# Staged weight loads, earlier LayerNorm statistics and a finer end in a two-layer encoder trunk

## The chip, the cores and the metric

The kernel runs on one core of a Trainium2 chip. The metric is the device time of one execution in microseconds (us). The kernel before took 2858.91 us in the median of three runs (2856.44 to 2863.42).

The core has a matrix engine (TensorE, PE), three engines for elementwise work (VectorE or DVE, ScalarE or ACT, GpSimd or POOL), and SyncE (SP), on whose queue this kernel issues its transfers. Each engine takes its instructions strictly in its own order, and waits on semaphores for the others.

## The reference

Two groups of rows, a prompt of 1024 tokens and a sample of 512, go through the same two layers of width 1024, and a last RMSNorm.

- Layer 0: RMSNorm, one input projection (`w_in_mix`), bidirectional retention with 4 heads beside differential attention with 8 heads, both gated, joined to 2048 columns, an output projection (`w_out_mix`, 2048 x 1024), and a residual.
- Layer 1: RMSNorm, a projection to three parts of 2048 (`w_in_conv`), then

```python
glu = a * jax.nn.sigmoid(b)
y = conv(glu, conv_w, width 31, depthwise) + conv_b
y = jax.nn.silu(layer_norm(y, cn_g, cn_b)) * jax.nn.silu(gate)
return x + y @ w_out          # w_out_conv, 2048 x 1024
```

The LayerNorm runs over the 2048 channels, so its statistics are known only when the last channel has been convolved.

## The kernel before, in words

All 1536 rows stay on one core. Matrix products keep the accuracy of float32 by splitting both factors into a high part, rounded to the matrix engine's format, and a low part, the rest: three matmuls (high by high, high by low, low by high) add into one PSUM tile of 128 x 512. ACT makes a high part by a cast, DVE or POOL the low part by a subtraction. That is true of weights and of activations.

The program is recorded by a layer that puts each instruction behind the ones it depends on and sorts by priority; `weave(spread(M), steps)` mixes a list of matrix work M with steps placed at fractions of its length (0 to 1). What the recording gives is a fixed order for each engine. A buffer of a pool is reused when all that reads it has run, so a load into one may stand in SP's queue and hold up all loads behind it.

The stages that the change touches, in order of time:

- **Attention output** (`oproj_steps`, L769 to L771). Each of twelve row tiles has a "slab" of 1 MB, the attention results, which SP loads. For four row tiles the first eight k (WA) are multiplied while the last head's job still runs, for the others (itemsB) behind it; the second eight k (WB) follow. `load_wout` loads the weights in pieces of 128 x 512 through three "wr" buffers, and splits each (L741 cast, L743 subtraction: DVE for WA, POOL for WB). "T1", "T2" and the like are big buffers of the head that serve as slabs.
- **Retention head** just before: vst are the rotated queries and keys (L384 to L386 on DVE), which free the PSUM tile "pp" for the next projection (L191 to L193). dmt are decay tables on DVE.
- **Convolution.** Sixteen channel tiles of 128 channels. `conv_setup` (L1209) loads the 31 weights of each channel through three "sg" buffers and transposes them on PE. The taps run on DVE (L1138). s1 and s2 hold the sums over channels of y and its square, added tile by tile on POOL (L1159, L1163).
- **LayerNorm.** `ln_cols` (L1264 to L1273) turns s1 and s2 by PE transposes, reduces them on DVE, and makes mu and vr, the reciprocal deviation (POOL's pow). `ln_rows` (L1281, L1282) spreads them back over the partitions, by four transposes each and ACT copies. Meanwhile PE runs the last gate projections, whose results ACT passes on with Silu (L1095, sg).
- **Output phase.** Three groups g of four row tiles t. Operand k of a group, z, is made by `z_make`: three DVE operations, Silu and cast on ACT, zl on POOL (L1315 to L1322). Five operands are kept (NZ). The products (L1364 to L1366, oc) run k by k over the four row tiles for the first KT of sixteen k, so that all eight PSUM banks fill at once, and then tile by tile for the rest, with the last RMSNorm behind each (`finish`, `finish_last`). The weights of `w_out_conv` (W1, W2) are loaded and split on POOL during group 0.

## Time and profile before

| what | us |
|---|---|
| median of three runs | 2858.91 (2856.44 to 2863.42) |
| profiled execution | 2858.97 |
| its span | 2857.0 |
| PE busy | 2801.6 (98%) |
| DVE, ACT, POOL busy | 1766.5, 1137.4, 1218.3 |

The span runs from the first to the last recorded instruction; 1.97 us lie around it. Start times count from the span's start. In a row of the timeline stand start, duration, engine, line, operation, output and input tiles, and in brackets the idle time ahead of it and what ended that. A row of waits tells who waited, for whom, how long in total, how often, and the longest.

### The profile page before, as it was taken

The numbers are of one execution on the slowest core, as the hardware profiler recorded it, in microseconds if no ns is written. First come the engines' busy times: TensorE is split into PE (matmuls) and PEld (weight loads), VectorE is DVE, ScalarE is ACT, GpSimd is POOL, SyncE is SP. The second block draws the span as 40 slices with busy tenths as digits, with TensorE's granted clock in tenths as the row PEclk, the third lists the DMA queues.
The fourth block names the chain that finished last, engine by engine and source line by source line (L and its number), as shares of the span: only waits on it lengthen the run. The fifth ranks groups of instructions, "written<-read, shape, count | busy, mean of one in ns | idle before, by whom it ended". The sixth has DMA issues, their size and how long they took to land.

```text
span 2857.0 us, 36862 instructions
## 1 busy us (share of the span) xinstructions
PE 2801.6 (98%) x13342; PEld 2314.7 (81%) x13342; DVE 1766.5 (62%) x3112; ACT 1137.4 (40%) x2124; POOL 1218.3 (43%) x1198
## 2 busy tenths in 40 slices
PE   7999999999999999999999999999999999999998
PEld 6788888888888778888878788788888888887787
DVE  4222336777777786665241143699899999965653
ACT  4233245555555665654332033333232323334321
POOL 4244343333333435555634000466565655556331
PEclk9999999999999999999999999999999999999999
DMA  4121222111111213333366653011221121255442
GB/s 132 46 64 51 59 67 76 55 52 55 55 55 51 81 51 95 98 102 98 98 209 208 209 177 113 25 56 58 65 72 59 51 81 63 74 173 178 161 144 81
DMA packets 283574, 264.32 MB, mean 93 GB/s; under 512 B 14636, under 2 KB 231908, under 8 KB 283264
## 3 DMA queue, kind: packets, MB, share of 16 engines
q1 hardware_dynamic: 283392, 261.96, 29.3%
q8 instruction: 105, 1.72, 0.2%
q14 instruction: 77, 0.63, 0.1%
HBM read 192.64 MB, written 69.27 MB: 92 GB/s over the span
## 4 chain that ended last, share of the span: by engine, by line
PE 89%; DMA 4%; DVE 2%; issue 2%; POOL 1%; ACT 1%; SPq 0%; DVEq 0%; POOLq 0%; ACTq 0%
PE pp L193 19%; PE pp L191 19%; PE pp L192 19%; PE pp L769 2%; PE pp L771 2%; PE pp L770 2%; PE sc L616 2%; PE sc L618 2%; PE tr L656 2%; PE oc L1366 2%; PE oc L1364 2%; PE oc L1365 2%; DMA wr<-in_w_out_mix 1%; PE o L673 1%; PE o L674 1%
## 5 line engine op out<-in xcount | busy, mean ns | idle before, releaser
L191 PE MATMUL pp<-hw,wh 128*128 128x512 f32 x2112 | 866.6, 410 | 1.3 <-DVE vst L386 0.9
L193 PE MATMUL pp<-hw,wl 128*128 128x512 f32 x2112 | 829.2, 393 | 0.0
L192 PE MATMUL pp<-hw,wh 128*128 128x512 f32 x2112 | 827.5, 392 | 0.0
L169 POOL TENSOR_TENSOR wl<-wr,wh 128x512 fp32r<-128x512 f32 x320 | 460.1, 1439 | 688.3 <-ACT wh L168 666.2
L193 PEld LDWEIGHTS pp<-hw,wl 128*128 128x128 f32 x2112 | 397.0, 188 | 88.1 <-issue 0.9
L191 PEld LDWEIGHTS pp<-hw,wh 128*128 128x128 f32 x2112 | 397.8, 188 | 77.8 <-issue 1.7
L192 PEld LDWEIGHTS pp<-hw,wh 128*128 128x128 f32 x2112 | 398.4, 189 | 73.1 <-issue 0.9
L168 ACT CAST wh<-wr 128x512 fp32r<-128x512 f32 x320 | 197.2, 616 | 552.2 <-PE pp L192 433.3
L620 DVE CUSTOM_DVE_ANT_0 st<-sc,W 128x512 f32<-128x512 f32 x320 | 208.9, 686 | 64.0 <-PE sc L618 54.4
L1138 DVE SCALAR_TENSOR_TENSOR acc<-xs,wS,acc 128x777 f32<-128x777 f32 x240 | 246.1, 1025 | 1.4
L1138 DVE SCALAR_TENSOR_TENSOR acc<-X,wE,acc 128x777 f32<-128x777 f32 x240 | 246.1, 1025 | 0.6
L631 ACT ACTIVATE st<-st,nm 128x1024 f32<-128x1024 f32 (+1 forms) x192 | 192.3, 1003 | 40.9 <-DVE nm L620 20.8
L1117 POOL TENSOR_TENSOR pa<-pa,ct 128x777 f32<-128x777 f32 x96 | 179.9, 1874 | 5.9
L659 ACT CAST ah<-tr 128x512 fp32r<-128x512 f32 x160 | 93.3, 584 | 171.8 <-PE tr L656 170.5
L193 PE MATMUL pp<-h2b,wl 128*128 128x512 f32 x384 | 152.4, 397 | 0.0
L191 PE MATMUL pp<-h2b,wh 128*128 128x512 f32 x384 | 152.4, 397 | 0.0
L192 PE MATMUL pp<-h2b,wh 128*128 128x512 f32 x384 | 151.9, 396 | 0.0
L593 POOL CAST qz<-T 64x128 fp32r<-64x128 f32 x192 | 57.3, 299 | 194.5 <-PE sc L618 189.0
L1138 DVE SCALAR_TENSOR_TENSOR acc<-X,wO,acc 128x777 f32<-128x777 f32 x112 | 115.4, 1031 | 25.4 <-ACT acc L1123 22.4
L1322 POOL TENSOR_TENSOR zl<-zy,zh 128x512 fp32r<-128x512 f32 x48 | 69.8, 1465 | 111.0 <-ACT zh L1321 86.7
L660 DVE TENSOR_TENSOR al<-tr,ah 128x512 fp32r<-128x512 f32 x160 | 109.8, 687 | 11.4 <-ACT ah L659 9.9
L647 DVE SCALAR_TENSOR_TENSOR st<-st,cf 128x1024 f32<-128x1024 f32 (+1 forms) x96 | 112.8, 1176 | 2.9
(262 smaller groups left out, 5064.1 us busy)
## 6 DMA issues: line engine op xcount, KB each, us to landing
wr<-in_w_in_mix SPq DMA_DIRECT2D x224, 256.0 KB, 2.9
wr<-in_w_in_conv SPq DMA_DIRECT2D x96, 256.0 KB, 2.8
slab<-acts SPq DMA_DIRECT2D x20, 1024.0 KB, 6.7
acts<-rhl SPq DMA_DIRECT2D x48, 256.0 KB, 2.9
acts<-ahl SPq DMA_DIRECT2D x96, 128.0 KB, 2.2
sgd<-sg SPq DMA_DIRECT2D x48, 256.0 KB, 3.4
zy<-yd SPq DMA_DIRECT2D x48, 256.0 KB, 3.9
sg<-sgd SPq DMA_DIRECT2D x48, 256.0 KB, 3.1
```

Source lines behind the costliest of these rows:

```text
L168: ACT.copy(h, t)
L169: POOL.tensor_tensor(out=l, in0=t, in1=h.bitcast(F32), op=ALU.subtract)
L191: PE.matmul(ps[g], a, hh[:, k, :], start=(half == 0 and k == 0), stop=False)
L192: PE.matmul(ps[g], a, hl[:, k, :], start=False, stop=False)
L193: PE.matmul(ps[g], b, hh[:, k, :], start=False, stop=(half == 1 and k == 3))
L620: DVE.tensor_tensor_reduce(out=U["st", qq, c][:, ns], in0=sc[c], in1=R["W"][:, off:off + 512], op0=ALU.add, op1=ALU.min, scale=1.0, scalar ...
L631: ACT.activation(out=st_, in_=st_, func=AF.Exp, scale=-1.0, bias=m, accum_out=U["Z", qq][:, c:c + 1])
L647: DVE.scalar_tensor_tensor(out=a, in0=U["st", qq, 1], scalar=cf, in1=a, op0=ALU.mult, op1=ALU.add)
L659: ACT.copy(ah, tp)
L660: DVE.tensor_tensor(out=al, in0=tp, in1=ah.bitcast(F32), op=ALU.subtract)
L1117: POOL.tensor_tensor(out=R["pa"], in0=R["pa"], in1=tmp, op=ALU.add)
L1138: DVE.scalar_tensor_tensor(out=dst, in0=x, scalar=wj, in1=acc, op0=ALU.mult, op1=ALU.subtract if first and nm == "S" else ALU.add)
```

## The change

It joins several edits:

1. `load_wout` is divided into load steps and split steps. WA has six staging buffers, WB uses nine idle ones (wr, wh, wl), the conv output weights use the buffers of z and then wh and wl. The first two pairs of k of W1 are split on DVE instead of POOL.
2. The convolution weights are loaded ahead into two "yv" buffers; `conv_setup` stands at 0.55 of its stretch instead of 0.4.
3. The last channel tile's sums are made on DVE. s1 and s2 lie in one tile.
4. `ln_cols` and `ln_rows` are placed earlier, with a higher priority; five operands z are made one by one between them, before the output phase. The s loads of z go to "wr".
5. The eight PSUM tiles of the output phase get names; the first row tile starts in the fifth.
6. KT is 13. The last two row tiles are finished by halves of 512 columns; in the last one the multiplication by final_g is done before the reciprocal root is known, and the two scalings run on ACT and DVE.

Some small tiles change names only. The diff, cut to its core:

```diff
@@ load_wout: from one step per pair of k to a load step and a split step @@
-    def load_wout(src, k0, pool, tag, pool2=None, tag2=None):
-        def one(kp):
+    def load_wout(src, k0, pool, tag, stage, pool2=None, tag2=None, first_eng=None):
+        W, raw = [], {}
+        eng = DVE if tag == "hw" and k0 == 0 else POOL
+        def load(kp):
+            def f():
+                for k in range(2):
+                    for c in range(2):
+                        r = raw[kp, k, c] = stage()
+                        r0 = (k0 + 2 * kp + k) * P
+                        SY.dma_start(out=r, in_=src[r0:r0 + P, c * 512:(c + 1) * 512])
+            return f
+        def split(kp):
+            e = first_eng if first_eng is not None and kp < 2 else eng
             def f():
...
-                        r = wpool.tile([P, 512], F32, name="wr", tag="wr", bufs=3)
-                        SY.dma_start(out=r, in_=src[r0:r0 + P, c * 512:(c + 1) * 512])
+                        r = raw.pop((kp, k, c))
                         ACT.copy(h[:, k, sl], r)
-                        eng.tensor_tensor(out=l[:, k, sl], in0=r, in1=h[:, k, sl].bitcast(F32), op=ALU.subtract)
+                        e.tensor_tensor(out=l[:, k, sl], in0=r, in1=h[:, k, sl].bitcast(F32), op=ALU.subtract)
...
+    class Stage:
+        def __init__(self, *tags):
+            self.tags, self.n = tags, -1
+        def __call__(self):
+            self.n += 1
+            pl, tg, bufs = self.tags[self.n % len(self.tags)]
+            return pl.tile([P, 512], F32, name=tg, tag=tg, bufs=bufs)
@@ w_out_mix, k 0 to 7 @@
-    WA, wa_steps = load_wout(A["w_out_mix"][0], 0, hw, "hw")
+    WA, wa_loads, wa_splits = load_wout(A["w_out_mix"][0], 0, hw, "hw", Stage((rpool, "wst", 6)))
-            ex = seq_of([f for _, f in wa_steps[0:2]], 0.1, 0.9)
+            ex = [(0.02, wa_loads[0]), (0.3, wa_splits[0]), (0.32, wa_loads[1]), (0.6, wa_splits[1]),
+                  (0.62, wa_loads[2])]
-    for _, f in wa_steps[2:4]:
-        f()
+    wa_splits[2]()
+    wa_loads[3]()
+    wa_splits[3]()
@@ w_out_mix, k 8 to 15 @@
-    WB, wb_steps = load_wout(A["w_out_mix"][0], 8, wbp, "wb")
+    idle = Stage((wpool, "wr", 3), (wpool, "wh", 3), (wpool, "wl", 3))
+    WB, wb_loads, wb_splits = load_wout(A["w_out_mix"][0], 8, wbp, "wb", idle)
-    weave(spread(chain_loads(itemsB)), seq_of([f for _, f in wb_steps], 0.1, 0.7))
+    weave(spread(chain_loads(itemsB)), seq_of(wb_loads, 0.02, 0.62), seq_of(wb_splits, 0.2, 0.8))
@@ sums of the last channel tile @@
-                POOL.tensor_tensor(out=s1, in0=s1, in1=y, op=ALU.add)
+                eng = DVE if t == NCT - 1 else POOL
+                eng.tensor_tensor(out=s1, in0=s1, in1=y, op=ALU.add)
...
-                    POOL.tensor_tensor(out=s2[:, r, :], in0=s2[:, r, :], in1=sq, op=ALU.add)
+                    eng.tensor_tensor(out=s2[:, r, :], in0=s2[:, r, :], in1=sq, op=ALU.add)
@@ convolution weights @@
+    craw = [cp.tile([P, 2, YW], F32, name="yv", tag="yv", bufs=2).rearrange("p r j -> p (r j)")[0:CONV_K, 0:1024]
+            for _ in range(2)]
+    for q in range(2):
+        SY.dma_start(out=craw[q], in_=A["conv_w"][0][:, q * 1024:(q + 1) * 1024])
...
-        for q in range(4):
-            craw = sgp.tile([CONV_K, 512], F32, name="sg", tag="sg")
-            SY.dma_start(out=craw, in_=A["conv_w"][0][:, q * 512:(q + 1) * 512])
-            for t in range(4):
-                c0 = (4 * q + t) * 31
-                PE.transpose(wps[:, c0:c0 + 31], craw[:, t * P:(t + 1) * P], ident[0:CONV_K, 0:CONV_K])
+        for t in range(NCT):
+            PE.transpose(wps[:, t * 31:t * 31 + 31], craw[t // 8][:, t % 8 * P:(t % 8 + 1) * P],
+                         ident[0:CONV_K, 0:CONV_K])
...
-        weave(spread(M), conv_steps(cur, old), [(0.4, conv_setup)] if t == 0 else [])
+        weave(spread(M), conv_steps(cur, old), [(0.55, conv_setup)] if t == 0 else [])
@@ between convolution and output phase @@
-    n = len(M) // 2
-    weave(spread(M[:n]), conv_steps(None, cur))
+    n = len(M) // 3
+    weave(spread(M[:n]), seq_of(cur[5], 0.0, 0.9) + [(0.92, cur[6])])
...
+    z_bufs = Stage((zp, "zh", NZ), (zp, "zl", NZ))
+    w_bufs = Stage((wpool, "wh", 3), (wpool, "wl", 3))
+    stage1 = lambda: (z_bufs if z_bufs.n < 7 else w_bufs)()
+    W1, w1l, w1s = load_wout(A["w_out_conv"][0], 0, w2p, "w2", stage1, h2b, "h2b", first_eng=DVE)
+    W2, w2l, w2s = load_wout(A["w_out_conv"][0], 8, hw, "hw", w_bufs)
...
-        s = sgp.tile([P, 512], F32, name="sg", tag="sg")
+        s = wpool.tile([P, 512], F32, name="wr", tag="wr", bufs=3)
...
+    def soon(f):
+        def g():
+            with tc.high_priority():
+                f()
+        return g
-    weave(spread(M[n:]), [(0.1, ln_cols), (0.3, z_first), (0.45, w1s[0][1]), (0.6, ln_rows(0)), (0.7, ln_rows(1)),
-                          (0.8, ln_rows(2)), (0.85, w1s[1][1])])
+    weave(spread(M[n:]), [(0.0, w1l[0]), (0.01, z_first), (0.02, w1l[1]), (0.08, soon(ln_cols)), (0.2, w1s[0]),
+                          (0.3, w1s[1]), (0.36, soon(ln_rows(0)))]
+          + seq_of([lambda m=m: pump(m - NZ + 1) for m in range(NZ)], 0.38, 0.85)
+          + [(0.55, soon(ln_rows(1))), (0.75, soon(ln_rows(2)))])
@@ output phase @@
-    oc = ps2.enter_context(tc.tile_pool(name="oc", bufs=8, space=PSUM))
+    oc = ps2.enter_context(tc.tile_pool(name="oc", bufs=1, space=PSUM))
+    oc_bank = {(t, c): f"oc{(2 * t + c + 4) % 8}" for t in range(4) for c in range(2)}
...
-    wload = [None, None] + [f for _, f in w1s[2:] + w2s]
+    wprep = {0: [w1l[2]], 1: [w1s[2], w1l[3]], 3: [w1s[3], w2l[0]], 5: [w2s[0], w2l[1]], 7: [w2s[1], w2l[2]],
+             9: [w2s[2], w2l[3]], 10: [w2s[3]]}
...
-    def finish_last(g, t):
+    def finish_halves(g, t, pool, tag, bufs, last):
...
+            if last:
+                xg.append(wpool.tile([P, 512], F32, name="wh", tag="wh", bufs=3))
+                DVE.tensor_tensor(out=xg[c], in0=xc[c], in1=gF[:, cs], op=ALU.mult)
...
-            DVE.scalar_tensor_tensor(out=xc[c], in0=xc[c], scalar=r, in1=gF[:, cs], op0=ALU.mult, op1=ALU.mult)
+            if not last:
+                DVE.scalar_tensor_tensor(out=xc[c], in0=xc[c], scalar=r, in1=gF[:, cs], op0=ALU.mult, op1=ALU.mult)
+            elif c == 0:
+                ACT.mul(xc[c], xg[c], r)
+            else:
+                DVE.tensor_scalar(out=xc[c], in0=xg[c], scalar1=r, scalar2=None, op0=ALU.mult)
...
-    KT = 12
+    KT = 13
...
-            if (g, t) == (2, 3):
-                finish_last(g, t)
+            if g == 2 and t >= 2:
+                pump(16 * g + KT)
+                finish_halves(g, t, *((wpool, "wl", 3, False) if t == 2 else (sgp, "sg", 3, True)))
```

How this moves instructions, at three places. On DVE, in the retention job before the attention output, the decay tables (dmt) and the rotation (L384 to L386); before:

```order
1880 L842 SCALAR_TENSOR_TENSOR dmt<-pk,lg,dmt 128x128 [waits DVE_49]
1881 L841 TENSOR_SCALAR dmt<-pk,lg 128x128 [waits Activation_49]
1882 L842 SCALAR_TENSOR_TENSOR dmt<-pk,lg,dmt 128x128 [waits DVE_49]
1883 L841 TENSOR_SCALAR dmt<-pk,lg 128x128 [waits Activation_49]
1884 L842 SCALAR_TENSOR_TENSOR dmt<-pk,lg,dmt 128x128 [waits DVE_49]
1885 L384 TENSOR_TENSOR vst<-pp,rope 128x512 [waits PE_49]
1886 L385 TENSOR_TENSOR vst<-pp,rope 64x512 [waits Pool_49]
1887 L386 TENSOR_TENSOR vst<-pp,rope 64x512
```

and with the change (wst are the staging buffers, hw the weights):

```order
1880 L860 SCALAR_TENSOR_TENSOR dmt<-pk,lg,dmt 128x128 [waits DVE_49]
1881 L859 TENSOR_SCALAR dmt<-pk,lg 128x128 [waits Activation_49]
1882 L752 TENSOR_TENSOR hw<-wst,hw 128x512 [waits DMAHW7_49,Activation_49]
1883 L860 SCALAR_TENSOR_TENSOR dmt<-pk,lg,dmt 128x128 [waits DVE_49]
1884 L859 TENSOR_SCALAR dmt<-pk,lg 128x128 [waits Activation_49]
1885 L860 SCALAR_TENSOR_TENSOR dmt<-pk,lg,dmt 128x128 [waits DVE_49]
1886 L752 TENSOR_TENSOR hw<-wst,hw 128x512 [waits DMAHW1_49,Activation_49]
1887 L752 TENSOR_TENSOR hw<-wst,hw 128x512 [waits DMAHW2_49,Activation_49]
1888 L384 TENSOR_TENSOR vst<-pp,rope 128x512 [waits PE_49]
1889 L385 TENSOR_TENSOR vst<-pp,rope 64x512 [waits Pool_49]
1890 L386 TENSOR_TENSOR vst<-pp,rope 64x512
```

Three weight splits (L752) now stand ahead of the rotation. On PE, at the LayerNorm, before (L1265 are the last column transposes, L1281 the row transposes, which wait for vr; between the two pieces stand 46 more matmuls):

```order
11022 L1265 MATMUL acc<-cpk,s_17183 128x128
11023 L1264 MATMUL acc<-cpk,s_17182 128x128
11024 L1265 MATMUL acc<-cpk,s_17183 128x128
11025 L193 MATMUL pp<-hw,wl 128x512
11026 L191 MATMUL pp<-hw,wh 128x512
```

```order
11073 L193 MATMUL pp<-h2b,wl 128x512
11074 L1281 MATMUL acc<-cpk,vr 128x128 [waits Pool_49]
11075 L1281 MATMUL acc<-cpk,vr 128x128 x3
11076 L1281 MATMUL acc<-cpk,mu 128x128 [waits DVE_49,PE_49]
```

and with the change (L1292 and L1308 are the same lines):

```order
11000 L1291 MATMUL acc<-cpk,s_17182 128x128
11001 L1292 MATMUL acc<-cpk,s_17182 128x128
11002 L192 MATMUL pp<-h2b,wh 128x512
11003 L193 MATMUL pp<-h2b,wl 128x512
11004 L191 MATMUL pp<-hw,wh 128x512
11005 L192 MATMUL pp<-hw,wh 128x512
11006 L193 MATMUL pp<-hw,wl 128x512 [waits Pool_49]
11007 L191 MATMUL pp<-hw,wh 128x512
11008 L192 MATMUL pp<-hw,wh 128x512
11009 L193 MATMUL pp<-hw,wl 128x512
11010 L1308 MATMUL acc<-cpk,vr 128x128 [waits Pool_49]
11011 L1308 MATMUL acc<-cpk,vr 128x128 x3
```

Eight matmuls stand between the column transposes and the first row transposes, where there were 49. On ACT, ahead of the output phase, before (L1095 are the gate copies; the last one stands behind casts and Silu steps of z):

```order
1455 L741 CAST h2b<-wr 128x512 [waits DMAHW5_49]
1456 L1321 CAST zh<-zy 128x512 [waits DVE_49] x2
1457 L1282 COPY s_17182<-acc 128x512 [waits PE_49]
1458 L1282 COPY s_17183<-acc 128x512 [waits PE_49]
1459 L1317 ACTIVATE zy<-zy,cnb,cng 128x512
1460 L1095 ACTIVATE sg<-pp 128x512 [waits DMAHW6_49,PE_49]
1461 L1317 ACTIVATE zy<-zy,cnb,cng 128x512
1462 L741 CAST h2b<-wr 128x512 [waits DMAHW6_49,PE_49]
1463 L1095 ACTIVATE sg<-pp 128x512 [waits DMAHW4_49,DMAHW0_49,PE_49]
```

and with the change (L1116 are the gate copies):

```order
1463 L751 CAST h2b<-wh 128x512 [waits DMAHW0_49]
1464 L1116 ACTIVATE sg<-pp 128x512 [waits DMAHW2_49,PE_49]
1465 L751 CAST h2b<-wl 128x512 [waits DMAHW1_49]
1466 L1348 ACTIVATE zy<-zy,cnb,cng 128x512 [waits DVE_49,Pool_49]
1467 L1116 ACTIVATE sg<-pp 128x512 [waits DMAHW5_49,PE_49]
1468 L751 CAST h2b<-wh 128x512 [waits DMAHW3_49,PE_49]
1469 L1116 ACTIVATE sg<-pp 128x512 [waits PE_49]
```

The operands' steps L1317, L1321 and the copies L1282 have left the rows ahead of the last gate copy; casts of weights (h2b) and one Silu of a later operand stand there.

58 lines of the change are left out of this document (27 added, 31 removed).

## The prediction

> **What bounds the kernel now.** I read the shares on the page first, then who TensorE (PE) waited for, then stretches around each wait, and last the timelines of the engines it waited for.
>
> ```profile
> span 2857.0 us, 36862 instructions
> PE 2801.6 (98%) x13342; PEld 2314.7 (81%) x13342; DVE 1766.5 (62%) x3112; ACT 1137.4 (40%) x2124; POOL 1218.3 (43%) x1198
> ```
>
> PE is busy for 98% of the span. The change leaves its multiplications as they are, so only PE's idle time can be won: 2857.0 - 2801.6 = 55 us, and what a reduced clock costs behind a stall. These are the waits (line, whom, us in total, times, longest):
>
> ```profile
> PE tr L255 <- DVE T L899: 10.5, 2, 9.6
> PE oc L1364 <- ACT sg L1095: 5.0, 1, 5.0
> PE tr L688 <- ACT osq L680: 4.5, 1, 4.5
> ...
> PE acc L1209 <- DMA sg<-in_conv_w: 3.7, 3, 1.7
> PE oc L1364 <- ACT zh L1321: 3.1, 1, 3.1
> PE pp L769 <- ACT hw L741: 2.2, 1, 2.2
> PE pp L769 <- DMA slab<-acts: 2.1, 1, 2.1
> ...
> PE tr L360 <- ACT vst L395: 1.3, 1, 1.3
> PE pp L769 <- DMA T<-acts: 1.3, 1, 1.3
> ```
>
> The first (start of the kernel) and the third (attention to value transposes) are in code that stays. The others sit where the change works. The stretches around them, with PE's busy time and matmul count, other engines, and the granted clock (the number before the DMA share):
>
> ```profile
> 1475.00:1490.00 15.00, 12.79 (x52) 9.96 (x51) 5.33 (x10) 1.89 (x4) 2.38 (x4) 0.89 0.74 232
> 1575.00:1582.00 7.00, 6.84 (x23) 5.46 (x24) 0.00 (x0) 0.00 (x0) 0.00 (x0) 0.76 0.85 249
> 1786.00:1800.00 14.00, 10.32 (x39) 7.52 (x39) 0.00 (x0) 1.27 (x3) 1.95 (x2) 0.76 0.03 11
> 2575.87:2582.00 6.13, 6.13 (x20) 4.96 (x21) 3.50 (x4) 3.02 (x5) 3.36 (x4) 0.74 0.59 192
> 2600.00:2648.00 48.00, 46.60 (x202) 37.55 (x200) 23.22 (x24) 17.41 (x28) 29.92 (x22) 1.00 0.48 147
> 2648.00:2656.00 8.00, 5.65 (x17) 4.24 (x18) 2.28 (x4) 2.28 (x4) 2.51 (x2) 0.79 0.33 97
> 2656.00:2700.00 44.00, 44.00 (x194) 35.92 (x193) 30.89 (x37) 16.40 (x26) 15.41 (x16) 1.00 0.59 195
> ```
>
> The last row gives the pace without waits: 44.00/194 = 0.227 us per matmul. Behind a wait of 2.1 us or more the clock falls: 0.11 x 15 = 1.65 us lost from 1475, 0.24 x 7 = 1.7 from 1575, 0.24 x 14 = 3.4 from 1786, 0.26 x 6.13 = 1.6 at 2576, 0.21 x 8 = 1.7 at 2648. So a wait of over 2 us costs itself and about 1.7.
>
> The Trainium skill ("TensorE: Matmul & The Clock Gate", section "What's actually happening") has the clock halve after at least one idle window of about 3.4 us. The trace disagrees: 2.1 us of idling were enough at 1575. By the page's rule a new wait of 2.8 us would keep the full clock, and the sum below would be 1.7 lower.
>
> **Attention output, first part (w_out_mix, k 0 to 7).** The weights were loaded through three shared "wr" buffers, each load waiting for a split. Now they have six buffers of their own, and the splits of the first half are recorded a job earlier.
>
> ```profile
> 1354.44 0.68 DVE L386 TENSOR_TENSOR vst<-pp,rope 64x512 f32<-64x512 f32 x1
> 1355.90 0.39 PE L191 MATMUL pp<-hw,wh 128*128 128x512 f32 x1
> ...
> 1471.99 6.42 DMA wr<-in_w_out_mix
> 1479.10 0.73 PE L769 MATMUL pp<-hw,T 128*128 128x512 f32 x2 [2.21 <-ACT hw L741]
> ```
>
> The load that started at 1471.99 lands after its work is due (1479.10 - 2.21 = 1476.9). With its own buffer it waits for no earlier split and lands near 1471, by the queue's order: minus 2.21 and its 1.65 of clock. The 1.29 of vst L395 (ACT stood behind a load queued after w_out_mix loads) goes too. Against this, three splits of 0.69 now stand ahead of the rope operations (L384 to L386) that free the PSUM tile which the matmul at 1355.90 overwrites: 2.07 on DVE, less the 0.8 us by which L386 ended early (1355.12), so +1.3. The 1.29 of T<-acts stays, since its slab is issued after the same matmul. Net -1.29 - 2.21 - 1.65 + 1.3 = **-3.85**; between -6.4 (no cost, T<-acts also cured: -1.29 - 2.21 - 1.65 - 1.29) and 0 (the moved loads land late).
>
> The Trainium skill ("SBUF — State Buffer", section "Who interferes with whom") says that VectorE and GpSimd exclude each other on a shared port pair. By it each moved split beside a POOL operation may take up to 1.29 longer, and this term would be -2.6 with one such wait.
>
> **Second part (k 8 to 15).**
>
> ```profile
> 1563.63 2.55 POOL L743 TENSOR_TENSOR wb<-wr,wb 128x512 fp32r<-128x512 f32 x2 [5.56 <-ACT wb L741]
> 1567.87 7.15 DMA slab<-acts
> 1575.16 0.47 PE L769 MATMUL pp<-hw,slab 128*128 128x512 f32 x1 [2.12 <-DMA slab<-acts]
> ```
>
> The slab of 1567.87 stood on SP's queue behind loads that waited for POOL's splits (the last ran to 1566.2). Nine staging buffers let the loads run ahead; the sixteen splits of 1.28 us then follow each other and end some 18 us earlier, and the slab can go when its buffer is free, near 1562.5. Landing 7.15 later, 1570, it is due at 1573. **-3.8** (2.12 and 1.7); between -3.8 and 0.
>
> **Convolution weights.** Four loads through three buffers made three waits, 3.7 us, and 3.4 of clock. Both halves are now fetched into idle "yv" buffers over 15 us before. The transposes stand in one block, behind which the mean's matmul waits for ACT copies with four matmuls (0.9 us) of cover; I charge 0.6. **-6.4**, between -7.1 and -3.
>
> **LayerNorm and the first output product.** The last channel's sums move from POOL to DVE, and the statistics' transposes move ahead.
>
> ```profile
> 2534.08 3.54 POOL L1159 TENSOR_TENSOR s<-s,yv 128x1554 f32<-128x1554 f32 x1
> 2545.18 2.81 DVE L1267 TENSOR_REDUCE col<-acc 128x4 f32<-128x512 f32 x4 [0.15 <-PE acc L1265]
> 2548.02 0.86 DVE L1268 TENSOR_SCALAR mu<-col 128x12 f32<-128x12 f32 x1
> 2549.58 2.29 POOL L1272 TENSOR_TENSOR vr<-vr,nh 128x12 f32<-128x12 f32 x1 [0.73 <-DVE vr L1271]
> 2551.90 1.25 DVE L1273 TENSOR_TENSOR mu<-mu,vr 128x12 f32<-128x12 f32 x1 [2.40 <-POOL vr L1272]
> 2571.32 0.62 ACT L1321 CAST zh<-zy 128x512 fp32r<-128x512 f32 x1 [2.29 <-DVE zy L1318]
> 2575.87 0.79 PE L1364 MATMUL oc<-w,zh 128*128 128x512 f32 x1 [4.99 <-ACT sg L1095]
> ```
>
> On DVE the sums take about 3.1 us (the 0.69 of 128x512 scaled to 1554 and 777 columns), where POOL took 3.54 for the first alone, and end near 2535.5; the transposes now come at 2538.8, 4.3 earlier, so that step is free. The chain behind them isn't: from the last transpose (reduced from 2547.3) to vr at 2551.87 it took 4.65 us, which 49 matmuls covered. Now 8 follow, 8 x 0.23 = 1.85. PE waits 4.65 - 1.85 = 2.8, and 0.3 more for mu and the copies; POOL has nothing else there, so mu should take nearer 0.2 than 1.25. With 1.7 of clock that is +4.8. Ends: 0 to +5.6, the latter with mu at 1.25.
>
> The output phase's first matmul waited 4.99 for ACT's last gate copy, which stood in ACT's queue behind casts that waited for DVE (2571.32). In the new order it still waits for that copy. I followed the queues by hand: five operands are made one by one, each three DVE operations of 0.69, two of ACT and one of POOL (1465 ns below), with loads of 3.9; all are ready by about 2570. The gate copy needs the last gate product and one more cast of 0.62 ahead of it: a wait of 1.0, without a fall of the clock. That removes 4.99 + 1.6 - 1.0 = 5.6. Net for the two **-0.8**, from -5.6 (no wait for statistics) to +5.6 (the dearest one, and the old first wait stays): most of what the first wait gives is spent on the statistics.
>
> **Rest of the output phase.**
>
> ```profile
> L1322 POOL TENSOR_TENSOR zl<-zy,zh 128x512 fp32r<-128x512 f32 x48 | 69.8, 1465 | 111.0 <-ACT zh L1321 86.7
> ...
> zy<-yd SPq DMA_DIRECT2D x48, 256.0 KB, 3.9
> ```
>
> Over 2600 to 2648, 202 matmuls at 0.227 are 45.9: 2.1 lost; over 2648 to 2656, 17 are 3.9: 4.1 lost. POOL makes each operand's low part (1465 ns) and also splits weights (1.29 each), and PE waited for both. The splits of the first two pairs of k now run on DVE ahead of the phase, and thirteen instead of twelve k are done before a tile's end. POOL then needs 2 x 1.3 + 1.47 = 4.1 per operand against 24 x 0.227 = 5.5 on PE. **-5.7** of 6.2; between -6.2 and -3.
>
> **The end.**
>
> ```profile
> 2849.22 1.28 DVE L1390 TENSOR_TENSOR sg<-oc,sg 128x512 f32<-128x512 f32 x2
> 2852.46 1.41 DVE L1396 SCALAR_TENSOR_TENSOR sg<-sg,nr,gF 128x512 f32<-128x512 f32 x2 [0.94 <-POOL nr L140]
> ```
>
> Both halves' additions ran after the last product (1.28); the first half's now comes earlier (-0.6), and the two scalings run side by side (-0.7). One more queued store gives 0.3 back: **-1.0**, between -1.6 and +0.5.
>
> The renamed tiles, the joined sums tile and named banks move nothing I can price: 0. **Sum:** -3.85 - 3.8 - 6.4 - 0.8 - 5.7 - 1.0 = -21.5. The profiled execution took 2858.97, almost the median of 2858.91, so 2837.4. All lower ends together give -31 (2828), all upper ones 0 (2859).
>
> **Rivals.**
>
> *The statistics hold (nothing new).* If no wait appears ahead of vr, 4.8 more are won: 2833, and 2828 at the other lower ends. For it: POOL idles there and its pow may be quicker. Against it: the 1.85 us of 8 matmuls are short of 2.29 + 0.86 alone.
>
> *Operands become the bound.* Loads for the fifth to eighth operand are chained through SP, DVE, ACT and POOL. If each takes 6.4 us like the load of 1471.99 instead of 3.9, three in a row add 7.5 ahead of the first output matmul, with 1.7 of clock: 2847. For it: DMA was busy for 0.59 there; against it stands the median of 3.9 itself.
>
> *It doesn't do what it says.* If the early loads only change their place in SP's queue, the gains of the two w_out_mix parts fail, the new rope wait stays, and T<-acts grows by 1.3 + 1.7. Then 2837.4 + 5.15 + 3.8 + 3 = 2849; with the rival above, 2858, no change.
>
> *Slower: slabs behind staged weights.* SP would stand at a staged load waiting for a buffer that four splits, 5.2 us, free; each slab behind it lands late by 5.2 less the 1 us it has to spare, and 1.7 of clock: 5.9. It decides from five of eight slabs on: 2837.4 + 3.8 + 29.5 = 2871. For it: that is how 1567.87 came late. Against it: nine buffers instead of three.
>
> **How the numbers follow.** Forecast 0.51, statistics hold 0.17, operands bound 0.17, doesn't do what it says 0.10, slabs late 0.05. A measurement tells 0.3% (8.6 us, so below 2850.3) from no change: the first two cases (0.68), 0.10 of the third and 0.04 of the fourth are faster, 0.82; the rest of these two, 0.13, is the same; slower 0.05. The range 2827 to 2850 leaves out the slower case and the upper ends.
>
> **What would show it.** In the new profile: no PE wait on hw L751, on a slab near 1570, on conv_w; a wait of about 2.8 on POOL's vr at the line of the row transposes with a clock of about 0.8 behind it; about 1 us at the first oc; no oc wait on zl or zh after. A PE wait near 1356 of about 1.3 shows the splits moved ahead. I am wrong if vr makes no wait, if the first oc waits over 3 us, or if slabs wait more than before.

## The result, and the profile after

The changed kernel took 2836.09 us in the median of four runs (2831.16 to 2837.09); the kernel before took 2858.16 (2856.44 to 2863.42) beside it. The ratio is 0.9916, with a 95% interval of 0.9899 to 0.9934: faster by 22 us, where 2837.4 had been predicted. The sum was right and most of its terms were not. The page of the changed kernel, in the profiled execution of 2837.09 us, has these first lines:

```profile
span 2835.1 us, 36862 instructions
PE 2778.9 (98%) x13342; PEld 2310.5 (81%) x13342; DVE 1770.3 (62%) x3126; ACT 1137.2 (40%) x2127; POOL 1191.8 (42%) x1187
```

PE does the same 13342 instructions, and its busy time fell by 22.7 us, from 2801.6. Its idle time did not fall: 2835.1 - 2778.9 = 56.2 us against 55.4 before. So the gain lies inside what the page calls busy: in the pace, that is the time from one matmul's start to the next where PE waits for nothing, and in the clock. The waits that the prediction counted were only exchanged for others. The waits of PE after (line, whom, us in total, times, longest):

```profile
PE oc L1408 <- ACT sg L1116: 6.5, 1, 6.5
...
PE acc L1308 <- POOL vr L1299: 3.5, 1, 3.5
PE pp L787 <- DMA T<-acts: 2.4, 1, 2.4
PE oc L1408 <- DVE zx L1415: 2.1, 1, 2.1
PE pp L191 <- DVE vst L386: 1.9, 2, 1.0
...
PE pp L787 <- DMA slab<-acts: 1.2, 3, 0.6
```

Gone are the waits on the convolution weights (3.7), on a cast of hw (2.2), on vst L395 (1.3) and on zh (3.1), and the slabs' fell from 2.1 to 1.2. New or longer are vr (3.5), the first product (6.5 instead of 5.0), T<-acts (2.4 instead of 1.3), the sums at a group boundary (2.1; zx holds a row tile's residual) and two small ones in the retention head (0.95 of the two on vst, and 0.6 on the masked scores smk). The stretches around them, with the granted clock ahead of the DMA share:

```profile
1465.00:1482.00 17.00, 14.58 (x63) 11.63 (x62) 8.25 (x13) 6.11 (x16) 6.88 (x9) 0.90 0.78 260
1772.00:1790.00 18.00, 18.00 (x95) 14.74 (x94) 1.27 (x4) 3.23 (x9) 4.68 (x5) 1.00 0.15 44
2521.00:2530.00 9.00, 5.52 (x35) 4.38 (x34) 6.30 (x14) 4.45 (x9) 3.95 (x2) 1.00 0.72 258
2548.00:2572.00 24.00, 17.48 (x71) 14.05 (x70) 13.37 (x11) 13.11 (x23) 18.81 (x14) 0.86 0.70 237
2645.00:2665.00 20.00, 17.90 (x73) 14.29 (x72) 12.79 (x16) 6.66 (x12) 7.33 (x9) 0.91 0.67 223
```

Where the convolution weights had cost 3.7 us, PE is now busy all through (1772 to 1790). The wait on vr (2521 to 2530) is there, but with a clock of 1.00. Now the stretches in which PE waits for nothing at all, of before and then of after, PE alone (length, busy and count, clock, DMA share, GB/s):

```profile
1810.00:2510.00 700.00, 700.00 (x3057) 1.00 0.19 63
2660.00:2820.00 160.00, 160.00 (x696) 1.00 0.46 147
```

```profile
1810.00:2510.00 700.00, 700.00 (x3090) 1.00 0.20 65
2660.00:2820.00 160.00, 160.00 (x707) 1.00 0.38 118
```

In the same 700 us of projections, on which the change has no edit, PE gets through 3090 instructions instead of 3057: from start to start, 229.1 ns each became 226.7, at the full clock in both. Over the stage that is 33 x 0.2267 = 7.5 us. The starts of matmuls of the same number in the two traces, after minus before, show what each stage brought (the rows end at matmul 6800, 7590, 8700, 8800, 12000, 12195, at the last one and at the end of the span):

| stretch of the program | predicted, us | measured, us |
|---|---|---|
| up to the last retention head | 0 | -1.8 |
| that head, and the attention output beside it (first part) | -3.85 | -1.7 |
| the attention output behind it (second part) | -3.8 | -3.2 |
| convolution weights | -6.4 | -8.0 |
| projections of the convolution stage | 0 | -7.7 |
| statistics and first output product | -0.8 | +4.9 |
| output phase | -5.7 | -6.3 |
| behind the last matmul | -1.0 | +0.6 |

(The rows add up to -23.2. The first matmul of the changed kernel's trace started 1.3 us later, which makes the 21.9 between the two spans.)

### The profile page after: what moved, and what is told of

Same layout as the page of the kernel before. It is cut to its first block, busy times and chain, and to the rows that moved or that the text cites. A ratio compares the mean times of both kernels' runs of the same rounds, so it can differ in the third digit from the quotient of the medians.

```text
span 2835.1 us, 36862 instructions
## 1 busy us (share of the span) xinstructions
PE 2778.9 (98%) x13342; PEld 2310.5 (81%) x13342; DVE 1770.3 (62%) x3126; ACT 1137.2 (40%) x2127; POOL 1191.8 (42%) x1187
## 3 DMA queue, kind: packets, MB, share of 16 engines
q8 instruction: 105, 1.72, 0.3%
```

## Experiments

### The pace: where the operands lie

What differs between the two programs also where the change has no edit is the place of tiles in SBUF. Three small tiles with names of their own (rssq, rr, cbs) became nssq and nr, which takes 384 bytes per partition out ahead of the big tiles; the joined tile s12 of 3200 columns is 320 bytes longer than s1 and s2 were. Nothing else moves them. So the description of the change, that some small tiles change names only, leaves this out. The starts per partition in the two built programs, in bytes modulo 512:

| tile | before | after |
|---|---|---|
| hw, wh, wl | 0 | 0 |
| h2b, T, wb, slab | 384 | 0 |
| w2, zh, zl | 64 | 0 |

So two runs exchange the addresses and leave every engine's order of instructions alone. The first is the kernel before, with the addresses of the change:

```diff
-                ssq = sm.tile([P, 1], F32, name="rssq")
+                ssq = sm.tile([P, 1], F32, name="nssq")
-                r = sm.tile([P, 1], F32, name="rr")
+                r = sm.tile([P, 1], F32, name="nr")
-        cbs = sm.tile([P, 1], F32, name="cbs")
+        cbs = sm.tile([P, 1], F32, name="nssq")
     s2 = lnp.tile([P, 2, YW], F32, name="s2")
+    lnp.tile([P, 80], F32, name="padl")
```

> This is the kernel before with nothing changed but where tiles lie in SBUF: the small tiles rssq, rr and cbs share the names nssq and nr (384 bytes less per partition ahead of the big tiles), and 320 unused bytes follow s2. All matmul operands then start at multiples of 512 bytes. Theory 1 (addresses): in the profiles the pace of matmuls outside waits fell from 229.1 to 226.7 ns in the convolution stage (some 3200 matmuls, 7.7 us), from 230.5 to 226.7 in the output phase (1152, 4.4 us) and by about 5 ns over some 500 matmuls of the attention output (2.6 us), so this kernel alone gains 14.7 us: 2843.5, with all the waits of before still there. Rival (the pace follows from less queueing or traffic in the changed order): the pace stays at 229 and the time at 2858, within 3 us.

It took 2846.34 us, ratio 0.9952 (0.9937 to 0.9967): 11.8 us for addresses alone. PE's stretches and two of its waits in this run:

```profile
1810.00:2510.00 700.00, 700.00 (x3090) 1.00 0.20 64
2660.00:2820.00 160.00, 160.00 (x707) 1.00 0.42 137
```

```profile
PE oc L1364 <- ACT sg L1095: 5.0, 1, 5.0
PE pp L769 <- DMA slab<-acts: 4.8, 2, 3.8
PE oc L1364 <- ACT zh L1321: 3.7, 1, 3.7
```

The counts are those of the change to the last instruction, and the waits of the kernel before are all still there, some of them longer (the slabs 4.8 instead of 2.1), so the pace alone is worth rather more than 11.8. The second is the change, with a pad that puts its tiles back to 384 (w2 and z too, which stood at 64 before):

```diff
     sm = root.enter_context(tc.tile_pool(name="sm", bufs=4))
+    sm.tile([P, 96], F32, name="pad", bufs=1)
```

> The changed kernel with 384 unused bytes ahead of the big tiles, so that h2b, the slabs, wb, w2 and z start 384 bytes past a multiple of 512 again, while hw, wh and wl stay on one. Theory 1 (addresses): the pace returns to about 229 ns in the convolution stage, with 232 for the matmuls that read h2b, and slows in the output phase for those that read hw; 12 to 15 us are lost: 2848 to 2851. So of the 22 us that the change gained, its waits give only about 7. Rival (order): 2836, the pace stays at 226.7.

2850.74 us, ratio 0.9975 (0.9965 to 0.9985, eight runs), with the counts of the kernel before:

```profile
1810.00:2510.00 700.00, 700.00 (x3057) 1.00 0.20 64
2660.00:2820.00 160.00, 160.00 (x698) 1.00 0.42 135
```

So all the change's edits to the order are worth 0.25%, some 7 us, and the addresses, which none of them mentions, 11.8 us in one kernel and 2850.74 - 2836.09 = 14.7 in the other. A third run asks for the rule, with other places: h2b, T, wb and slab at 256, the weights w2 and the operands z at 320 modulo 512.

```diff
     sm = root.enter_context(tc.tile_pool(name="sm", bufs=4))
+    sm.tile([P, 64], F32, name="pad", bufs=1)
-    s12 = lnp.tile([P, 3200], F32, name="s12")
+    s12 = lnp.tile([P, 3216], F32, name="s12")
```

> The changed kernel with 256 unused bytes ahead of the big tiles and 64 more behind the sums: h2b starts 256 bytes past a multiple of 512, z and w2 start 320 past one, hw, wh and wl on one. If matmuls run at 226.7 ns only where both operands start at the same place modulo 512, then h2b in the convolution stage (256 apart) and both hw (320 apart) and h2b (64 apart) in the output phase slow to 229 to 234 ns while w2 there (0 apart) stays at 227. If a step of 256 bytes is enough, h2b in the convolution stage stays at 226.7. If only offsets from a multiple of 512 count, w2 slows too. The time: 2848 to 2855 in the first case.

A single execution took 2836.73 us, not the 2848 and more of the first case. The second case held for the projections, which kept the full pace with h2b 256 bytes away from its partner; the output phase lost it:

```profile
1810.00:2510.00 700.00, 700.00 (x3090) 1.00 0.20 65
2660.00:2820.00 160.00, 160.00 (x691) 1.00 0.35 113
```

Sorted by the places of a matmul's two operands, the mean time from one start to the next is, over the kernels above:

| the two places, modulo 512 | ns |
|---|---|
| 0 and 0; 384 and 384; 64 and 64; 320 and 320 | 226 to 229 |
| 256 (h2b) and 0 (wh) | 226.7 |
| 384 and 64 | 226 to 232, mean 229 |
| 384 and 0; 64 and 0; 320 and 0; 320 and 256 | 232 to 234 |

Full pace where both operands start at the same place modulo 256, some 6 ns (2.6%) more per matmul where they don't, and about 2.5 for 384 and 64. One pair stays outside: the scores of two T tiles, both at 384, took 231 before, and 227 with both at 0 or both at 256 (medians). Why the place matters was not tested. The Trainium skill ("SBUF — State Buffer", section "SBUF: two separate sides") says that PE never waits on anyone; that is about the other engines, and the rows above, with 3 to 7 ns per instruction, are about PE's own two operands.

### The first output product

The prediction gave it a wait of 1.0; it waits 6.52. The timeline of the changed kernel (start, duration, engine, line, operation), VectorE, GpSimd, ScalarE and PE:

```profile
2537.44 1.79 DVE L1346 TENSOR_TENSOR zy<-zy,s 128x512 f32<-128x512 f32 x1
2539.26 1.67 DVE L1347 TENSOR_TENSOR zy<-zy,s 128x512 f32<-128x512 f32 x1
2540.85 0.68 DVE L1349 TENSOR_TENSOR zy<-zy,wr 128x512 f32<-128x512 f32 x1
...
2555.57 1.63 DVE L1347 TENSOR_TENSOR zy<-zy,s 128x512 f32<-128x512 f32 x1
...
2536.94 3.44 POOL L1353 TENSOR_TENSOR zl<-zy,zh 128x512 fp32r<-128x512 f32 x2 [9.96 <-ACT zh L1352]
...
2557.30 0.81 ACT L1348 ACTIVATE zy<-zy,cnb,cng 128x512 f32<-128x512 f32 x1 [3.90 <-DVE zy L1347]
...
2559.00 0.59 ACT L1116 ACTIVATE sg<-pp 128x512 f32<-128x512 f32 x1
...
2559.65 0.80 PE L1408 MATMUL oc<-w,zh 128*128 128x512 f32 x1 [6.52 <-ACT sg L1116]
```

A VectorE operation of this size takes 0.68 where GpSimd is idle (2540.85) and 1.6 to 1.8 where a split runs on it. Nine were so lengthened. The Silu of the eighth operand (2557.30) waited for the last of them, and the gate copy that frees the bank (2559.00) stood behind it on ScalarE. This is the rule that the prediction cited for the first part of the attention output and did not apply here. Two runs take the two halves of this apart. The first moves the gate copies: the Silu of operands from the sixth on, and four casts of weights, are queued behind the last gate copy.

```diff
+            with (tc.issue_after(last_gate[0]) if tg == "h2b" and kp == 3 else ExitStack()): ACT.copy(h[:, k, sl], r)
+        with (tc.issue_after(last_gate[0]) if m >= NZ else ExitStack()): ACT.activation(out=y, in_=y, func=AF.Silu, ...)
```

> The changed kernel, with the Silu steps of the sixth and later operands and the casts of the fourth weight pair queued on ACT behind the last gate copy. Theory 2: the first output matmul waited 6.5 us because the gate copy stood on ACT behind a Silu that waited for VectorE, whose operations took 1.7 us beside GpSimd's instead of 0.69. Then the wait shrinks to about 1 us and the 6.8 us of half clock behind it (3.4 us) go: 8 to 9 us faster than the changed kernel, 2827.5. Rival (the operands themselves are late, or weights on GpSimd): the wait stays with another releaser and the time at 2834 to 2836.

2837.72 us, ratio 0.9924 (0.9910 to 0.9939). The first product waits 0.75, as the theory had it, and the time did not move:

```profile
PE oc L1408 <- DVE zx L1415: 6.5, 2, 3.9
...
PE acc L1308 <- POOL vr L1299: 3.5, 1, 3.5
...
PE oc L1408 <- ACT sg L1116: 0.7, 1, 0.7
```

What was won is spent again at the next group boundary, 90 us later: by the starts of matmuls this run is 5.9 us ahead of the changed kernel before that boundary and 1.4 us behind it. The second run takes GpSimd away: the low parts of the first five operands are split on VectorE, five instructions more for the engine that was late.

```diff
-        POOL.tensor_tensor(out=l, in0=y, in1=h.bitcast(F32), op=ALU.subtract)
+        (DVE if m < NZ else POOL).tensor_tensor(out=l, in0=y, in1=h.bitcast(F32), op=ALU.subtract)
```

> The changed kernel, with the low parts of the first five operands of the output product split on VectorE instead of GpSimd: five instructions of 0.69 us more for VectorE, none beside it on GpSimd until the slab of weights. Theory: VectorE's elementwise instructions took 1.6 to 1.8 us instead of 0.69 because GpSimd's splits ran beside them; some nine of them were so lengthened, by 9.5 us, ahead of the Silu that stands in front of the last gate copy. With the splits gone they take 0.69 us, 3.1 us are added, and the first product waits 0.3 to 2.5 us instead of 6.5; the time is 2831 to 2834, if nothing later takes it back. Rival: VectorE is slow there for another cause (DMA traffic at 220 GB/s, or ScalarE beside it): the instructions keep 1.6 us, the wait grows to about 9 us, and the time is 2838 to 2841.

```profile
2547.99 0.68 DVE L1353 TENSOR_TENSOR zl<-zy,zh 128x512 fp32r<-128x512 f32 x1
...
2552.75 1.37 DVE L1346 TENSOR_TENSOR zy<-zy,s 128x512 f32<-128x512 f32 x1 [2.87 <-DMA zy<-yd]
2554.15 1.65 DVE L1347 TENSOR_TENSOR zy<-zy,s 128x512 f32<-128x512 f32 x1
```

Every elementwise instruction takes 0.68 or 0.69 until GpSimd's splits of weights begin at 2549.78, and 1.37 and 1.65 beside them. From 2536 to 2549 the transfers (share 0.83 instead of 0.75) and ScalarE (8.5 us busy instead of 6.8) did even more than in the changed kernel, so what lengthens VectorE here is GpSimd beside it. The wait fell to 3.53, not to the 0.3 to 2.5 expected: a load (2.87) ended last. The time, 2831.87, ratio 0.9905 (0.9891 to 0.9920), is within the range given, but its interval overlaps that of the change, so the total alone would not have told it. Nor is all of it this wait's: the wait of 2.1 us at the group boundary is gone in this run too, without an edit there.

### The group boundary

A group boundary is where PE goes from the last row tile of a group to the first of the next. With 13 of 16 indices ahead, the last three of a row tile are 18 matmuls, 4.08 us. The changed kernel at its second boundary:

```profile
2648.89 1.29 DVE L1415 TENSOR_TENSOR zx<-oc,zx 128x512 f32<-128x512 f32 x2 [1.51 <-DMA zx<-x1d]
...
2653.86 1.29 DVE L1415 TENSOR_TENSOR zx<-oc,zx 128x512 f32<-128x512 f32 x2 [0.23 <-DMA zx<-x1d]
...
2654.61 0.52 PE L1408 MATMUL oc<-w,zh 128*128 128x512 f32 x1 [2.10 <-DVE zx L1415]
```

A tile finishes some 5 us after the one before it, and the next group needs its bank. The 2.1 us are a close race: the wait is missing in four other builds of the change without an edit there (the two with pads, where PE is slower in this phase, the one with low parts on VectorE, and the one with the old convolution loads). Two guesses at why were tried on top of the run with the gate copies first. One is KT 12, that is 5.4 us per tile:

```diff
-    KT = 13
+    KT = 12
```

> The same as the kernel with the gate copies first, and KT back at 12. Theory 3: the wait of 2.1 us at the start of the second row group, for the addition of a finished tile that itself waited for its x load, comes from KT 13: a tile's last k then last 4.1 us, and its finishing (two additions, square, root, scaling, store, next load through two buffers) about 5. With KT 12 they last 5.5 us; the wait and 1.7 us of clock go: 3.8 us faster than the kernel with the gate copies first, 2823.7. Rival: with KT 12 the wait of before for an operand (3.1 and 0.7 us, on the cast of z) comes back in its place: no gain, 2827 to 2828.

2834.66 us, ratio 0.9909 (0.9892 to 0.9925). The wait on zx is gone and the wait on an operand is back (zh, 2.9 us with 6.83 us of half clock), as in the kernel before: the rival held for the wait, and the interval overlaps that of the run with the gate copies first.

The other keeps KT 13, with the third and fourth tile of every group by halves, in buffers of their own, so that no addition waits for the load of its residual:

```diff
-            if g == 2 and t >= 2:
+            if t >= 2:
...
-                finish_halves(g, t, *(... if t == 2 else (sgp, "sg", 3, True)))
+                finish_halves(g, t, *(... if t == 2 else (sgp, "sg", 3, g == 2)))
```

> The kernel with the gate copies first (KT 13), and the third and fourth row tile of every group finished by halves of 512 columns, with their x in the idle buffers wl and sg, so that no x load waits for an earlier tile's store. Theory 3, mended: the first output wait went to 0.75 us, but two waits for additions at the start of the second group grew to 2.6 and 3.9 us, because PE came there earlier while the additions wait for x loads through two buffers. Then both and the 1.7 us of clock go: 8 us faster than the kernel with the gate copies first (2837.7), so 2829.5. Rival: the operands are next: a wait on the cast of z or on zl of 3 us and more takes their place, as with KT 12, and the time stays at 2834 to 2838.

2836.23 us, ratio 0.9925 (0.9909 to 0.9942): a miss. The longest wait is 4.92 now, again on a sum, with 6.83 us of half clock; of the two waits together, 6.5 us, 5.5 stay. So the loads were not the main thing that was late. On this base the rows' transposes lost their priority, so that 20 to 30 matmuls stand between them and the statistics:

```diff
-                          (0.3, w1s[1]), (0.36, soon(ln_rows(0)))]
+                          (0.3, w1s[1]), (0.36, ln_rows(0))]
-          + [(0.55, soon(ln_rows(1))), (0.75, soon(ln_rows(2)))])
+          + [(0.55, ln_rows(1)), (0.75, ln_rows(2))])
```

> The same as the kernel with tiles by halves, and the row transposes of the LayerNorm without the higher priority: 20 instead of 8 matmuls stand between the last column transposes and the first row transposes, 30 and 24 between the rows. Theory 4: PE's 3.5 us wait for vr is the chain DVE, POOL, 5.3 us from the last transpose, less what covers it: with 20 matmuls (4.5 us) it falls below 1 us, and 2.7 us are gained, 4.4 where the clock fell behind the wait. From 2829.5 that is 2825 to 2827. Rival: the operands start later by as much, and the first output product waits 3 us and more for them: 2829 or above.

2835.27 us, ratio 0.9919 (0.9904 to 0.9933). The wait on vr is 0.75 instead of 3.48, and the total does not show it: in this build the waits on ox, the rows of the attention output, are 3.0 instead of 0.7. Next, the splits of the first w_out_mix weights were held behind the work recorded ahead of them on VectorE:

```diff
+    with (tc.issue_after(<the VectorE instruction recorded before>) if e is DVE and k0 == 0 and tag == "hw" else ExitStack()):
+        e.tensor_tensor(out=l[:, k, sl], in0=r, ...)
```

> The same as the kernel with rows later, and VectorE's splits of the first w_out_mix weights kept behind the instruction recorded before them, so that they no longer run in the earlier retention job ahead of the rotation. Theory 5: these splits cost PE the waits at 1356 and 1363 (0.8 to 2.1 and 0.6 us) and some more while VectorE shares its port with GpSimd: 1.5 to 2.7 us are gained, 2823.5. Rival: they then come late for the attention output, and the wait for hw of 2.2 us and 1.7 of clock returns: 2827 to 2830.

2832.60 us, ratio 0.9909 (0.9895 to 0.9924). The waits near 1356 and 1364 are gone (1.6 us), and one of 0.6 on hw has come. The time lies outside both forecasts. What stays largest is the boundary, and this run's VectorE shows its cause:

```profile
2645.26 3.40 DVE L1445 SCALAR_TENSOR_TENSOR wl<-wl,nr,gF 128x512 f32<-128x512 f32 x2 [0.94 <-POOL nr L140]
2648.59 1.27 DVE L1435 TENSOR_TENSOR sg<-oc,sg 128x512 f32<-128x512 f32 x2
```

The last tile's additions (2648.59) stand on VectorE behind the scaling of the tile before, which waits for its statistic and then takes 1.7 instead of 0.7 a piece beside GpSimd. VectorE takes its work in order: two additions (1.28), 1.6 to 2.2 us for the statistic, a scaling (1.28) make 4.2 to 4.8 per tile, against 4.08 of matmuls. So it falls behind from tile to tile. To test that, each scaling was recorded behind the next tile's additions:

```diff
+        def scale():
+            DVE.scalar_tensor_tensor(out=x, in0=x, scalar=r, in1=gF, op0=ALU.mult, op1=ALU.mult)
+            SY.dma_start(out=xrow2(out_p, out_s, tile_of(4 * g + t)), in_=x)
+        scales.append(scale)
...
+            while len(scales) > (g < 2 and t < 3):
+                scales.pop(0)()
```

> The kernel of the run with the weight splits not ahead (2832.6 us), and the scaling of an output tile, with its store, is queued on VectorE behind the additions of the next tile (in the first two groups of output rows; the last group is as before). Theory: at the second group boundary the last additions are late (4.92 us of TensorE, and 6.83 us of half clock, 3.4 us) because VectorE takes its work in order and the scaling of a tile waits some 2.2 to 2.9 us for its statistic, so that a tile costs it 1.28 + 2.2 + 1.28 = 4.8 us, against 4.1 us of matmuls with 13 indices ahead. With the scaling behind the next sums no product waits over 0.7 us at the two boundaries, no half clock stands there, and the time is about 2832.6 - 4.9 - 3.4 = 2824. Rival: what is late is the splitting beside it (the scaling by halves took 3.40 us for two beside GpSimd), not the order: a wait of over 2 us stays at a boundary and the time is 2829 to 2833.

2825.97 us, ratio 0.9884 (0.9867 to 0.9900). But the edit did less than it says: the recording layer, which orders by its own priorities, put the scalings of the two whole tiles back ahead of the additions and let only one half of the third past. The boundary's wait fell from 4.92 to 3.26 and kept its half clock. The rest of the gain on the run before (a wait of 2.6 us on ox, 1.1 on a slab) is not of this edit; such waits differ from build to build where nothing near them was edited. So the order was fixed by a dependence:

```diff
-                scales.pop(0)()
+                with (tc.issue_after(last_add[0]) if g < 2 else ExitStack()): scales.pop(0)()
```

> The kernel of the run with the scaling behind the next sums (2826.0 us), in which the recorder that orders the instructions by its own costs had kept the two whole tiles' scalings ahead of the next additions and moved one instruction only. Here the order is fixed: on VectorE both additions of an output tile stand ahead of the scaling of the tile before it, in the first two groups. Theory: the additions at the second boundary are late (3.26 us, and 6.83 us of half clock, 3.4 us) because they stand behind scalings that wait 1.6 to 2.2 us for their statistic. Ahead of them they end within a microsecond of their matmuls; no product waits over 0.8 us at a boundary, no half clock stands there, and the time is 2826 - 3.3 + 0.5 - 3.4 = 2820. Rival: the order of the additions is not what is late, but the low parts of the operands that VectorE and GpSimd make in the same microseconds: a wait of over 1.5 us stays at the boundary, on the sums or on an operand (zh or zl), and the time is 2824 to 2828.

2820.06 us (2818.88 to 2825.55), ratio 0.9860 (0.9842 to 0.9878): the theory's 2820, and faster than both kernels, by 38 us than the one before and by 16 than the change. The interval still touches that of the run before it (0.9867), so the boundary itself is the evidence; the execution profiled is the slowest of the four, 2825.55, with waits of 2.0 on ox and 1.8 on hw and a half clock of 3.41 us behind each, and whether the three others lack these was not seen. VectorE and PE at the boundary:

```profile
2642.34 1.28 DVE L1438 TENSOR_TENSOR sg<-oc,sg 128x512 f32<-128x512 f32 x2
2643.53 3.29 DVE L1449 SCALAR_TENSOR_TENSOR wl<-wl,nr,gF 128x512 f32<-128x512 f32 x2
```

```profile
2640.00:2660.00 20.00, 20.00 (x90) 16.55 (x89) 16.91 (x23) 8.45 (x17) 7.95 (x10) 1.00 0.79 263
```

The scaling still takes 3.29 beside GpSimd, and now no matmul waits for it. Counted from the same matmul (number 12500), VectorE begins the first tile's additions when it did in the run before (11.9 and 12.1 us behind it), and the last tile's two 6.6 and 7.7 us earlier; so it is the order that ends the wait.

### Convolution weights

This term was taken from the changed kernel alone, by giving it the old loads at the old place:

```diff
-            PE.transpose(wps[:, t * 31:t * 31 + 31], craw[t // 8][:, t % 8 * P:(t % 8 + 1) * P], ...)
+        for q in range(4):
+            craw = sgp.tile([CONV_K, 512], F32, name="sg", tag="sg")
+            SY.dma_start(out=craw, in_=A["conv_w"][0][:, q * 512:(q + 1) * 512])
...
-        ... [(0.55, conv_setup)] if t == 0 else [])
+        ... [(0.4, conv_setup)] if t == 0 else [])
```

> The changed kernel, with the convolution's weights loaded and transposed again as in the kernel before (four loads through a ring of three buffers inside the first channel tile's weave, at 0.4). The operands stay at their places. Theory: the waits of the kernel before on these loads come back (1.7 + 1.4 us, with the clock halved behind them), 6.4 us by the prediction's term, up to 8 by the comparison of the two traces: 2842 to 2845. Rival: what the comparison shows there is the pace of the operands alone, and the loads are hidden in the new order: 2836 to 2838.

A single execution took 2845.32 us, with the waits back:

```profile
PE acc L1234 <- DMA sg<-in_conv_w: 4.1, 3, 2.1
```

4.1 us and a half clock of 6.83 us (3.4) are 7.5 us; by the starts of matmuls this stretch takes 8.1 us more than in the changed kernel. Other places add and take away: 1.8 before it, with longer waits on ox, some 2 by the first output product, where the clock now falls behind vr, and -3.8 at the group boundary, whose wait is missing here. The rival (hidden loads) falls.

## Why the prediction came out right, and where it failed

**The total.** -21.5 was forecast and -22.1 measured, by two errors that cancel: that the total came out is luck. The waits were to give all of it; without the addresses they gave some 7 (2850.74). The term "the renamed tiles, the joined sums tile and named banks move nothing I can price: 0" was -12 to -15. It was the step that failed most: the rename was read as a change of names, and the diff's shorter layout was not looked at. Nor was the pace of before read rightly: 44.00/194 = 0.227 counts two matmuls that had begun ahead of the stretch; from start to start it ran at 0.2295, the projections at 0.229, and the pace was not looked up for each pair of tiles, where 227 to 234 ns would have shown. The two runs with exchanged addresses, by the starts of matmuls against the kernel before, part the two causes (one execution each, so small waits of other places are in the rows):

| stretch of the program | predicted, us | order alone (tiles at 384) | places alone (kernel before, tiles at 0) |
|---|---|---|---|
| up to the last retention head | 0 | -0.2 | -1.6 |
| attention output, first part | -3.85 | +0.9 | 0.0 |
| attention output, second part | -3.8 | -2.3 | +0.4 |
| convolution weights | -6.4 | -7.8 | -0.7 |
| projections of the convolution stage | 0 | 0.0 | -7.7 |
| statistics and first output product | -0.8 | +6.3 | -0.3 |
| output phase | -5.7 | -6.4 | -3.1 |
| behind the last matmul | -1.0 | +0.3 | 0.0 |

**Convolution weights, -6.4.** Right in mechanism and nearly in size: 8.1 by the run that undid it, -8.0 between the traces. The 0.6 charged for ACT's copies did not come.

**Attention output, -3.85 and -3.8.** The waits named are gone (hw L741, vst L395, the slab near 1575). But "the 1.29 of T<-acts stays" failed: 2.4 with a half clock of 3.41 us behind it (0.90 over the first stretch above), 1.7 to 3.3 in the other runs of this order. And +1.3 for the splits ahead of the rope was two waits, 0.95 and 0.62:

```profile
1353.01 1.29 DVE L752 TENSOR_TENSOR hw<-wst,hw 128x512 fp32r<-128x512 f32 x2
...
1356.45 0.47 PE L191 MATMUL pp<-hw,wh 128*128 128x512 f32 x1 [0.95 <-DVE vst L386]
...
1356.73 5.49 DVE L752 TENSOR_TENSOR hw<-wst,hw 128x512 fp32r<-128x512 f32 x4
...
1364.17 0.70 PE L476 MATMUL o<-T,smk 128*128 128x256 f32 x2 [0.62 <-DVE smk L458]
```

The first came for the reason given: the three splits ahead of the rope took their plain 0.65 to 0.68 each. The second stands behind four more splits that took 5.49 us, 1.4 each, beside GpSimd; there the sentence applied that the sum did without. So the waits of this part, 6.4 us with their clock before, are 5.7 now, and the -3.85 came only to -0.7; the rest of the measured -1.7 is pace, as is about 1 us of the second part's -3.2, and no term had it.

**Statistics, +4.8.** The wait came where it was put, 3.48 for the 2.8 + 0.3 forecast:

```profile
2524.32 2.66 POOL L1299 TENSOR_TENSOR vr<-vr,nh 128x12 f32<-128x12 f32 x1 [0.31 <-DVE vr L1298]
2527.02 0.17 DVE L1300 TENSOR_TENSOR mu<-mu,vr 128x12 f32<-128x12 f32 x1 [2.18 <-POOL vr L1299]
2527.04 0.65 PE L1308 MATMUL acc<-cpk,vr 128*128 128x128 f32 x4 [3.48 <-POOL vr L1299]
```

The guess for mu (0.2 instead of 1.25) was right at 0.17. "With 1.7 of clock" failed in this execution, where the clock stayed; in the seven other profiles with the same 3.48 us it fell (the last section tells why).

**First output product, -5.6.** Failed: "each three DVE operations of 0.69" were 1.6 to 1.8 beside GpSimd, and the wait of 1.0 was 6.52 with 6.83 us of half clock. The prediction had named this as its own disproof (over 3 us). Moving the gate copies makes the wait 0.75, so the place was right and the price of VectorE wrong.

**Output phase, -5.7.** Of the 6.2 us counted as lost, 0.7 were pace: from 2600 to 2648 PE idled for 1.4, not 2.1. The waits on zh and zl went, and the boundary's 2.1 with 3.4 us of half clock came: a tile was costed by GpSimd's 4.1 against PE's 5.5 per operand, and not by VectorE's 4.2 to 4.8 against 4.08 per finished tile. The -6.3 measured contains some 4 us of pace (1152 matmuls at 226.7 instead of 230.4 ns).

**The end, -1.0.** It was +0.6. The two scalings do run side by side:

```profile
2828.28 0.68 DVE L1435 TENSOR_TENSOR sg<-oc,sg 128x512 f32<-128x512 f32 x1
2828.99 0.69 DVE L1439 TENSOR_TENSOR wh<-sg,gF 128x512 f32<-128x512 f32 x1
...
2830.85 0.72 ACT L1447 ACTIVATE sg<-wh,nr 128x512 f32<-128x512 f32 x1 [1.13 <-POOL nr L140]
```

But the second half's addition starts 2.1 us behind the last matmul (2826.15), since on VectorE the scaling of the tile before, the first half's addition and its multiplication by final_g stand ahead of it; in the kernel before both additions had ended 1.9 us behind the last matmul.

**Rivals.** None of the four took the place of the forecast. What came was a fifth thing, that the waits move: of the runs that cured one wait more each, the gate copies, the halves and the later rows left the time between 2835.3 and 2837.7, and only with the boundary cured too did it fall to 2820. In part the second rival came, in its effect and not by its cause: the first output product waited 6.5, not for loads but for VectorE beside GpSimd.

## What to carry to other kernels

A change of layout is a change of time: look up where the operands of the big matmuls start before and after an edit that only renames or joins tiles, and compare the count of matmuls in long stretches without waits. Cost an engine by what runs beside it, and a finishing step by its whole chain on one in-order engine against the matmuls that cover it. And when a cured wait returns at the next step, cure the last one of the chain before judging any of them.

## What the runs showed of the hardware

**The clock looks at fixed stretches.** The half-clock stretches last 3.41 or 6.83 us, and in the changed kernel they begin at 1470.52, 2555.96 and 2654.95: whole multiples of 3.413 us apart. A wait of 2.42 us ending at 1470.73, with 2.2 us inside one stretch of that grid, lowered the clock, and so did the 2.10 us ahead of 2654.61, wholly inside one. The 3.48 us on vr did not: a boundary of the grid (2525.24) cuts them into 1.7 and 1.8. In the seven other profiles with the same 3.48 us (the pads, the gate copies, KT 12, the halves, the late convolution weights, the low parts on VectorE) 2.1 us or more fell into one stretch of the grid, and the clock was lowered. Over all profiles here, behind the first 40 us and at full clock, 1.96 us and more of idling inside one stretch always lowered it, less than 1.72 never did, and in between both occur. The grid lies otherwise in each profile. So a wait's cost of clock is a matter of where it falls. The Trainium skill ("TensorE: Matmul & The Clock Gate", section "What's actually happening") calls the window free-running, with 3413 ns, and the trace agrees; its "after ≥1 idle window" the trace does not bear out, since some 2 us of idling within a window were enough.

**VectorE beside GpSimd.** 0.69 became 1.6 to 1.8 in the changed kernel, and 1.37 and 1.65 in the run with the low parts on VectorE; the Trainium skill ("SBUF — State Buffer", section "SBUF: two separate sides") has the two exclude each other on a shared port pair when VectorE's instruction has two inputs in SBUF and GpSimd's reads SBUF, and the trace agrees.

**The pace of matmuls by operand places** is told with its runs above. What stays open is its cause, the one pair of T tiles that does not fit, and whether a step smaller than 256 bytes would do.
